# A two-stage Strassen MLP behind an attention and SSD block: sums and transposes laid into the output projection, the first and last two up pairs run product by product, low parts of W_down taken from PSUM, left sides of the down projection in half tiles

## The chip, the cores and the metric

The kernel runs on one core of a Trainium2 chip. The metric is the device time of one execution in microseconds (us), the median of several runs.

## The reference

One decoder block on x of 1024 rows and 1024 columns, all in float32. Only the end of it matters here:

```python
h1 = x + mix @ w_out                        # output projection, K = 2048
h  = rmsnorm(h1, norm_mlp_w)
u  = jnp.square(jax.nn.relu(h @ w_up))      # 1024 -> 4096
h2 = h1 + u @ w_down                        # 4096 -> 1024
y  = rmsnorm(h2, norm_final_w)
```

`mix` is the concatenation of the outputs of 16 state-space heads and 16 attention heads.

## The kernel before

All large products run as three passes of a rounded format: an operand is split into a high part (a cast on ScalarE) and a low part (the operand less its high part, a subtraction on VectorE or GpSimd), and high by high, high by low and low by high are added up in PSUM. `parts` (line 1179) is this split: `ac.copy` writes the high part, `low_by.tensor_tensor(... ALU.subtract)` the low part.

Both MLP products use one level of Strassen's method in Winograd's form: seven products in place of eight, with sums of quarters ahead and behind. Tokens are halved into rows 0 to 3 and 4 to 7 (tiles of 128 rows), K and columns are halved too.

- **Output projection** (`oproj_jobs`, line 827). Four groups `eg` of four K tiles; for each token tile and each half of the columns 12 matmuls into a bank `po`, then VectorE adds the bank to `h1`. The matmuls are yielded one by one by the generator `body`, and `fill` (line 321) draws them; `after(n, fn)` puts a function behind n further draws.
- **Norm and right sides of up** (lines 1152 to 1190 and 1312 to 1345). `norm_rows` makes `hn` for four rows, `turn` transposes it on TensorE into a bank `nt_m`, `quarter` splits a quarter, and from the two token halves come `b11`, `b21`, `b22` and the sums `t1` to `t4` (tiles `g_...`, for which `ta`, `tb` and `cc` are steps). All of it stands behind the last `po`; pair 0's first two products stand between the halves.
- **Up** (lines 1199 to 1360). 16 pairs `p`; each loads two blocks of W_up, makes its seven left sides (`up_split`: sums `us_...` on GpSimd, splits `uo_...` on ScalarE and VectorE) and runs seven products of 12 matmuls of 128x512 each. Banks `pu_a`, `pu_b`, `pu_c` collect them; `relu` and square give the four quarters of u, GpSimd makes the three sums and one difference that the next stage needs as left sides, and all seven go to DRAM (`uc_d`), tile `uc` by tile.
- **Down** (lines 1363 to 1510). 8 chunks of 2 pairs by 4 row positions i are 32 slots. A slot (`down_mm`) runs seven products of 6 matmuls. Two slots ahead, `down_in` loads the left sides of both pairs (`ul`, 896 columns, 448 KB by the SyncE queue), casts them on ScalarE (`uh`) and subtracts in place; GpSimd does that for i = 0 to 2 and VectorE for i = 3. `down_split` makes the seven right sides of a pair of W_down: sums `ds_t` on GpSimd, then `parts` on ScalarE and VectorE (`do_t` for sums, `do_b` for raw quarters of `wsd`). There are 22 buffers for them, 14 of which a chunk uses, so that most of a chunk's splits wait until the last slot of the chunk ahead frees their buffers. Each product is read from its bank (`pn_a` to `pn_d`) by VectorE, which adds it to `h1b` or `acc`; `pn_a`, `pn_b` and `pn_c` are used twice in a slot, and the second product into a bank waits for the read of the first.
- Behind the last chunk `final` squares, scales and writes the rows.

Each engine works through its own queue in order. The order in a queue comes from a scheduler that takes the program's order and the engines' occupation into account; only stretches between `kept.add("t")` and `kept.discard("t")` hold TensorE to the program's order. Buffers and banks belong to tags with fixed counts (`BUFS` and `PBUFS`, lines 103 and 105: eight banks as d 2, s 3, t 2, v 1).

Of the kernel before, what the change touches and what calls it, by code (L numbers as in the profile page):

```python
# [45 lines left out]
def tile_hymba_block(  # L46
# [780 lines left out]
    def oproj_jobs(eg):  # L827
# [337 lines left out]
    def turn(nts, k, th):
        pt = ps(("s", "t")[k % 2], f"nt_m_{th}_{k}")
        for ti in range(4):
            te.transpose(pt[:, ti * P:(ti + 1) * P], nts[ti][:, k * P:(k + 1) * P], ident)
        return pt
# [13 lines left out]
    cc = []
    nts = norm_rows(0)
    for k in range(HK):
        cc.append(sb("q", [P, 2, 512], F32, f"cc{k}"))
# [55 lines left out]
    banks = {}  # L1242
    t1s = {}

    def up_first(p):

        a = banks[p, "a"] = ps("d", f"pu_a{p}")
        up_prod(a, p, "a11", "b11", True)
        t1s[p] = sb(("y", "y", "vt")[p % 3], [P, 512], F32, f"ut1_{p}")
        ac.copy(t1s[p], a)  # L1250

    def up_second(p):
        up_prod(banks[p, "a"], p, "a12", "b21", False)

    def up_rest(p, between):
        a = banks[p, "a"]
        t1 = t1s[p]
        st = [sb(("p", "p", "ws")[(4 * p + j) % 3], [P, 4, 2, P], F32, f"uc{p}_{j}") for j in range(4)]

        def view(m):  # L1260
            j = UM.index(m)
            return st[j // 2][:, :, j % 2, :]

        def v3(ap):
            return ap.rearrange("p (i t) -> p i t", t=P)

        def tmp(nm):
            return sb("t", [P, 512], F32, f"u{nm}_{p}")

        def act(dst, src):  # L1270
            ac.activation(dst, src, AF.Relu)
            ac.activation(dst, dst, AF.Square)

        b = ps("s", f"pu_b{p}")
        up_prod(b, p, "s2", "t2", True)
        u2 = tmp("u2")
        ve.tensor_tensor(out=u2, in0=b, in1=t1, op=ALU.add)
        if between is not None:
            between()
        ac.activation(view("a11"), v3(a), AF.Relu)  # L1280
        ac.activation(view("a11"), view("a11"), AF.Square)
        up_prod(b, p, "s3", "t3", False)
        u3 = tmp("u3")
        ve.tensor_tensor(out=u3, in0=b, in1=t1, op=ALU.add)
        c = ps("t", f"pu_c{p}")
        up_prod(c, p, "s1", "t1", True)
        ve.tensor_tensor(out=u3, in0=c, in1=u3, op=ALU.add)
        up_prod(b, p, "a22", "t4", False)
        ac.activation(u3, u3, AF.Relu)
        ac.activation(view("a22"), v3(u3), AF.Square)  # L1290
        c21 = tmp("c21")
        ve.tensor_tensor(out=c21, in0=b, in1=t1, op=ALU.add)
        ac.activation(c21, c21, AF.Relu)
        ac.activation(view("a12"), v3(c21), AF.Square)
        up_prod(c, p, "s4", "b22", False)
        ve.tensor_tensor(out=u2, in0=c, in1=u2, op=ALU.add)
        act(u2, u2)
        a21 = v3(u2)
        gp.tensor_tensor(out=view("s3"), in0=view("a11"), in1=a21, op=ALU.subtract)
        gp.tensor_tensor(out=view("s1"), in0=a21, in1=view("a22"), op=ALU.add)  # L1300
        gp.tensor_tensor(out=view("s2"), in0=view("s1"), in1=view("a11"), op=ALU.subtract)
        gp.tensor_tensor(out=view("s4"), in0=view("a12"), in1=view("s2"), op=ALU.subtract)
        for j in range(4):
            n = min(2, 7 - 2 * j)
            sy.dma_start(out=uc_d[p][:, :, 2 * j:2 * j + n, :], in_=st[j][:, :, 0:n, :])
# [232 lines left out]
```

## Time and profile before

| | us |
|---|---|
| median of 3 runs | 1770.62 (1768.61 to 1771.44) |
| profiled execution, its own time | 1766.85 |
| its span | 1765.0 |
| TensorE busy in the span | 1632.2 (92%) |
| VectorE busy | 1211.0 (69%) |
| ScalarE busy | 763.7 (43%) |
| GpSimd busy | 779.0 (44%) |

In the profile the engines are PE (TensorE matmul), PEld (TensorE weight load), DVE (VectorE), ACT (ScalarE), POOL (GpSimd) and SP (SyncE, which issues the DMAs). All instructions are issued through one wrapper, so every row names line 85 and groups are told apart by their tiles. In a timeline the bracket behind a row is the idle time ahead of it and what ended that. The output projection ends at 1027.1, up at 1366.5, down at 1753.8.

### The profile page before, as it was taken

What the parts mean: (1) busy time and instruction counts of PE and PEld (TensorE: products, weight loads), DVE (VectorE), ACT (ScalarE), POOL (GpSimd) and SP (SyncE); (2) the same over time, 40 slices, a digit from 0 to 9 for tenths busy, and PEclk for the clock granted to TensorE, in tenths of its full rate; (3) what the DMA queues carried; (4) which work ended last, traced back from release to release, by engine and by line L of the source; (5) the groups of instructions that cost most, each with busy time, mean ns of one, the idle gap of its engine ahead of it and who ended that gap; (6) DMA issues with size and microseconds to landing.
All of it is one profiled execution on the core that took longest, in us unless ns stands there. A gap on an engine that the chain in (4) does not pass through costs nothing.

```text
span 1765.0 us, 22987 instructions
## 1 busy us (share of the span) xinstructions
PE 1632.2 (92%) x7994; PEld 1349.6 (76%) x7994; DVE 1211.0 (69%) x2082; ACT 763.7 (43%) x1610; POOL 779.0 (44%) x788
## 2 busy tenths in 40 slices
PE   7999898899999999999999968999999599888896
PEld 7887687778888888887888857888887477666775
DVE  5666867567777776777855466655655888888864
ACT  4223444335555555556411255455455333333333
POOL 4233553354333443443201145544544855556547
PEclk9999999999999999999999989999999799999998
DMA  5122334431112111103432322554555633333223
GB/s 172 42 58 63 93 84 100 83 82 32 35 34 46 35 35 32 44 27 125 148 105 86 107 84 74 165 155 138 160 162 195 228 122 132 131 116 123 102 96 121
DMA packets 171068, 175.38 MB, mean 99 GB/s; under 512 B 43364, under 2 KB 143928, under 8 KB 170952
## 3 DMA queue, kind: packets, MB, share of 16 engines
q1 hardware_dynamic: 169784, 173.12, 32.6%
q8 instruction: 63, 1.03, 0.3%
q0 software_dynamic: 1024, 0.53, 0.1%
q14 instruction: 53, 0.43, 0.1%
q10 hardware_dynamic: 144, 0.26, 0.0%
HBM read 127.15 MB, written 46.73 MB: 99 GB/s over the span
## 4 chain that ended last, share of the span: by engine, by line
PE 63%; DVE 11%; DMA 8%; issue 5%; ACT 5%; POOL 4%; SPq 0%; POOLq 0%; DVEq 0%; ACTq 0%
PE po L85 9%; PE pj_qk L85 8%; PE pu_b L85 7%; PE pj_v L85 5%; DMA eb<-cum_d 5%; PE pu_c L85 5%; PE pu_a L85 4%; PE s L85 4%; PE o L85 3%; PE tp L85 3%; PE pj_x L85 3%; PE pn_a L85 3%; PE pn_b L85 2%; DVE do_t L85 2%; PE pn_c L85 2%
## 5 line engine op out<-in xcount | busy, mean ns | idle before, releaser
L85 POOL TENSOR_SCALAR p<-p,rs 128x512 f32<-128x512 f32 (+2 forms) x144 | 102.9, 720 | 247.1 <-DVE rs L85 135.9
L85 PE MATMUL po<-wh_o,yy 128*128 128x512 f32 x512 | 161.8, 393 | 0.4 <-DVE k L85 0.4
L85 ACT ACTIVATE p<-s,mx 128x512 f32<-128x512 f32 (+1 forms) x192 | 110.4, 579 | 89.6 <-DVE mx L85 69.3
L85 ACT CAST uh<-ul 128x896 fp32r<-128x896 f32 x64 | 60.2, 942 | 179.0 <-DMA ul<-uc_d 166.2
L85 POOL TENSOR_TENSOR ul<-ul,uh 128x896 fp32r<-128x896 f32 x48 | 112.9, 2361 | 54.0 <-ACT uh L85 53.7
L85 DVE TENSOR_TENSOR pl<-tp,ph 128x512 fp32r<-128x512 f32 x192 | 105.9, 553 | 38.1 <-ACT ph L85 34.9
L85 ACT CAST ph<-tp 128x512 fp32r<-128x512 f32 x192 | 91.7, 478 | 70.0 <-PE tp L85 69.7
L85 PEld LDWEIGHTS po<-wh_o,yy 128*128 128x128 f32 x512 | 95.4, 188 | 19.4 <-DVE k L85 0.7
L85 PE MATMUL pj_qk<-hh,wl_qk 128*128 128x512 f32 x256 | 106.2, 415 | 0.0
L85 PE MATMUL pj_qk<-hl,wh_qk 128*128 128x512 f32 x256 | 105.9, 414 | 0.0
L85 PE MATMUL pj_qk<-hh,wh_qk 128*128 128x512 f32 x256 | 103.4, 404 | 0.0
L85 PE MATMUL s<-k,q 68*128 68x512 f32 (+7 forms) x384 | 101.9, 347 | 1.1 <-ACT p L85 0.9
L85 PE MATMUL po<-wl_o,yy 128*128 128x512 f32 x256 | 100.6, 393 | 0.0
L85 PE MATMUL pu_b<-g_t,uo_s 128*128 128x512 f32 x384 | 93.9, 394 | 4.0 <-DVE uu L85 4.0
L85 PE MATMUL tp<-ident,p 128*128 128x128 f32 x576 | 95.2, 273 | 1.2 <-POOL p L85 1.2
L85 PE MATMUL pu_a<-g_b,uo_a 128*128 128x512 f32 x384 | 94.5, 396 | 1.4 <-ACT ut L85 1.4
L85 DVE TENSOR_TENSOR do_t<-ds_t,do_t 128x512 fp32r<-128x512 f32 x64 | 91.6, 1433 | 5.6 <-ACT do_t L85 5.5
L85 PE MATMUL pz<-wh_z,hh 128*128 128x256 f32 (+1 forms) x256 | 76.9, 300 | 14.0 <-DVE z L85 11.4
L85 DVE TENSOR_TENSOR uo_s<-us_s,uo_s 128x512 fp32r<-128x512 f32 x64 | 61.9, 968 | 38.9 <-ACT uo_s L85 38.7
L85 PEld LDWEIGHTS pu_b<-g_t,uo_s 128*128 128x128 f32 x384 | 73.0, 191 | 20.0 <-DVE uu L85 3.5
L85 PEld LDWEIGHTS tp<-ident,p 128*128 128x128 f32 x576 | 72.6, 140 | 20.0 <-POOL p L85 2.6
L85 PEld LDWEIGHTS pu_a<-g_b,uo_a 128*128 128x128 f32 x384 | 73.1, 191 | 17.5 <-ACT ut L85 2.3
(293 smaller groups left out, 4721.4 us busy)
## 6 DMA issues: line engine op xcount, KB each, us to landing
ul<-uc_d SPq DMA_DIRECT2D x64, 448.0 KB, 4.0
uc_d<-uc SPq DMA_DIRECT2D x48, 512.0 KB, 3.2
ws_up<-in_w_up_dram SPq DMA_DIRECT2D x32, 512.0 KB, 3.8
wsd<-in_w_down_dram SPq DMA_DIRECT2D x32, 512.0 KB, 3.4
eb<-cum_d SPq DMA_DIRECT2D x16, 512.0 KB, 8.6
ws_qk<-in_w_in_dram SPq DMA_DIRECT2D x32, 256.0 KB, 3.6
wso<-in_w_out_dram SPq DMA_DIRECT2D x16, 512.0 KB, 3.4
yr<-yT_d SPq DMA_DIRECT2D x32, 256.0 KB, 2.7
```

Of the source, the lines that this page charges most:

```text
L85: i = call(*args, **kw)
```

## The change

- The last group of the output projection is drawn with other work between its matmuls. `norm_row` makes a row's norm as soon as its second half has been added; from row 3 on, the transposes and splits of the first token half (`left`, eight pieces), six splits of W_up for pairs 0 and 1, and the first half of the right sides' transposes and sums (`right_turn`, `right_sums`) are put behind counted draws. TensorE is held to program order from the middle of this group to the end of pair 1, and `po` has two banks there instead of five.
- Pairs 0 and 1 run product by product together, in the order p1, p2, p6, p7, p5, p4, p3; the sums t1 to t4 are made between them, t1's and t3's low parts on DVE. The last two pairs run together too, with p5 ahead of p7.
- A pair's result a22 is no longer copied into a `uc` tile but written to DRAM from the tile it is made in (`uu3`).
- From the second chunk on, a right side of W_down is cast twice on ACT: once into SBUF (the high part) and once into a PSUM bank `hb` (tag s); the low part is SBUF operand less PSUM bank, on DVE. `pn_b` moves to the two banks t and `pn_c` to d.
- The left sides come as half tiles `ui` (products 0 to 3 and 4 to 6 of a slot; high and low part in one tile), in a ring of 10 tiles over the tags q, p and ws, and all their low parts are made on POOL.

Its core:

```diff
@@ up
-    drain()
...
+    oproj_jobs(EG - 1, row)
+    fill(2 * (EG - 2) * NT * 3 * EG + NT * 3 * EG)
+    kept.add("t")
+    drain()
+    for p in range(2):
+        ups[p] = Up(p, "dts")
+    ups[0].p1()
+    ups[1].p1()
+    for k in range(HK):
+        right_turn(k, 1)
+    for k in range(HK):
+        right_sums(k, 1)
+        parts(gtile("t2", k), ta[k][:, 1, :], ve)
+    ups[0].p2()
+    ups[1].p2()
+    ups[0].p6()
+    ups[1].p6()
...
+        parts(gtile("t3", k), tb[k], ve)
...
+        parts(gtile("t1", k), ta[k][:, 0, :], ve)
...
+    ups[0].p7()
+    ups[1].p7()
...
+    for p in range(2, NPAIR - 2):
         up_load(p)
...
+    tails = [Up(p) for p in (NPAIR - 2, NPAIR - 1)]
...
+    for m in ("p1", "p2", "p6", "p5", "p7", "p4", "p3"):
+        for u in tails:
+            up_split(u.p, OP[m], True)
+        for u in tails:
+            getattr(u, m)()
@@ down_split
-            parts(o, src[m], ve)
+            if p < CP:
+                parts(o, src[m], ve)
+            else:
+
+                hb = ps("s", f"hb_{m}_{p}")
+                ac.copy(hb.bitcast(F32R), src[m])
+                ac.copy(o[:, 0], src[m])
+                ve.tensor_tensor(out=o[:, 1], in0=src[m], in1=hb, op=ALU.subtract)
@@ down_in
-            sy.dma_start(out=r32(lo), in_=uc_d[p][:, i])
-            ac.copy(hi, r32(lo))
-            (gp if i % 4 < 3 else ve).tensor_tensor(out=lo, in0=r32(lo), in1=r32(hi), op=ALU.subtract)
-            us_in[p, i] = hi, lo
+        for a, b in ((0, 4), (4, 7)):
+            for p in range(c * CP, (c + 1) * CP):
+                o = sb(uring[nu[0] % len(uring)], [P, 2, b - a, P], F32R, f"ui{p}_{i}_{a}")
+                nu[0] += 1
+                sy.dma_start(out=r32(o[:, 1]), in_=uc_d[p][:, i, a:b])
+                ac.copy(o[:, 0], r32(o[:, 1]))
+                gp.tensor_tensor(out=o[:, 1], in0=r32(o[:, 1]), in1=r32(o[:, 0]), op=ALU.subtract)
+                us_in[p, i, a // 4] = o
@@ down_mm
-        bb = ps("s", f"pn_b{nm}")
+        bb = ps("t", f"pn_b{nm}")
...
-        bc = ps("t", f"pn_c{nm}")
+        bc = ps("d", f"pn_c{nm}")
```

**Where instructions move.** At the start of up, on DVE, `g_t1` and `g_t3` are the low parts of the sums t1 and t3, `tb` the sum t3 itself, `uu2` the read of a p6 product. Before, k by k, each t3 follows its t2:

```order
L85 SCALAR_TENSOR_TENSOR ta1_10577<-nt_m_1_1_10570,prm_92,cc1_10390 128x512
L85 SCALAR_TENSOR_TENSOR ta1_10577<-nt_m_1_5_10579,prm_92,ta1_10577 128x512
L85 SCALAR_TENSOR_TENSOR tb1_0_10588<-nt_m_1_5_10579,prm_92,c12_1_10575 128x512
L85 TENSOR_TENSOR g_t2_1_10585<-ta1_10577,g_t2_1_10585 128x512
L85 TENSOR_TENSOR g_t3_1_10591<-tb1_0_10588,g_t3_1_10591 128x512
```

After the change, between the reads of pair 0's and pair 1's p6 and the product p7 (which needs t3):

```order
L85 TENSOR_TENSOR uu2_0_10682<-pu_b0_10669,ut1_0_10580 128x512
L85 TENSOR_TENSOR g_t1_2_10739<-ta2_10526,g_t1_2_10739 128x512
L85 TENSOR_TENSOR g_t1_3_10744<-ta3_10545,g_t1_3_10744 128x512
L85 TENSOR_TENSOR uo_s1_1_10796<-us_s1_1_10794,uo_s1_1_10796 128x512
L85 TENSOR_TENSOR uu2_1_10697<-pu_b1_10684,ut1_1_10595 128x512
L85 SCALAR_TENSOR_TENSOR tb0_3_10699<-nt_r4_10476,prm_92,cc0_10309 128x512
L85 SCALAR_TENSOR_TENSOR tb1_3_10709<-nt_r5_10500,prm_92,cc1_10348 128x512
L85 SCALAR_TENSOR_TENSOR tb2_3_10719<-nt_r6_10521,prm_92,cc2_10385 128x512
L85 TENSOR_TENSOR g_t3_0_10701<-tb0_3_10699,g_t3_0_10701 128x512
```

The parts of t1, which p5 uses, now stand ahead of those of t3, which TensorE's queue uses first, in p7.

On SP, where up gives over to down: `uc_d15` is the write of pair 15's left sides, `ui1_1_0` the load of pair 1's first half for the second slot. Before (`ul1_1` is the load for that slot):

```order
L85 DMA ul0_0_13101<-uc_d0_10447 128x896
L85 DMA uc_d15_10462<-uc15_0_12929 512x1x256
L85 DMA uc_d15_10462<-uc15_1_12930 512x1x256
L85 DMA uc_d15_10462<-uc15_2_12931 512x1x256
L85 DMA ul1_0_13106<-uc_d1_10448 128x896
L85 DMA ul1_1_13120<-uc_d1_10448 128x896
```

After:

```order
L85 DMA uc_d14_9461<-uc14_2_12933 512x1x256
L85 DMA uc_d15_9462<-uc15_0_12790 512x1x256
L85 DMA uc_d15_9462<-uc15_1_13000 512x1x256
L85 DMA uc_d15_9462<-uc15_2_12949 512x1x256
L85 DMA ui0_1_0_13095<-uc_d0_9447 128x512
L85 DMA ui1_1_0_13099<-uc_d1_9448 128x512
L85 DMA ui0_1_4_13103<-uc_d0_9447 128x384
L85 DMA ui1_1_4_13107<-uc_d1_9448 128x384
```

Slot 0's loads have moved ahead of the last writes (further up in the queue), slot 1's all stand behind them.

On DVE, in the last slot of chunk 3 and the first of chunk 4, before:

```order
L85 TENSOR_TENSOR do_t1_9_14387<-ds_t1_9_14385,do_t1_9_14387 128x512
L85 TENSOR_TENSOR h1b_3_13129<-h1b_3_13129,pn_a3_3_14319 128x512
L85 TENSOR_TENSOR do_t2_9_14397<-ds_t2_9_14395,do_t2_9_14397 128x512
L85 TENSOR_TENSOR h1b_7_13131<-h1b_7_13131,pn_b3_3_14327 128x512
L85 TENSOR_TENSOR do_t3_9_14392<-ds_t3_9_14390,do_t3_9_14392 128x512
```

After:

```order
L85 TENSOR_TENSOR do_t1_9_14571<-ds_t1_9_14569,hb_t1_9_14572 128x512
L85 TENSOR_TENSOR h1b_3_13119<-h1b_3_13119,pn_a3_3_14495 128x512
L85 TENSOR_TENSOR do_t3_9_14578<-ds_t3_9_14576,hb_t3_9_14579 128x512
L85 TENSOR_TENSOR do_t2_9_14585<-ds_t2_9_14583,hb_t2_9_14586 128x512
L85 TENSOR_TENSOR h1b_7_13121<-h1b_7_13121,pn_b3_3_14503 128x512
```

The subtractions and the reads take turns as before; the second operand of a subtraction is the bank `hb`.

## Rows read from the trace of the kernel before

**Rows 1.** Busy time by stage: stretch in us, its length, then busy us (and records) of PE, PEld, DVE, ACT and POOL, the granted clock, the share of the DMA engines and GB/s.

```profile
1027.10:1100.00 72.90, 54.15 (x234) 42.95 (x233) 50.50 (x62) 44.31 (x78) 37.90 (x31) 0.88 0.20 65
1100.00:1340.00 240.00, 240.00 (x1060) 198.75 (x1059) 142.68 (x165) 121.74 (x202) 121.59 (x88) 1.00 0.50 154
...
1366.50:1394.00 27.50, 8.58 (x19) 5.52 (x20) 25.01 (x18) 12.43 (x21) 25.76 (x16) 0.57 0.72 268
1394.00:1704.00 310.00, 276.68 (x1159) 220.46 (x1159) 257.48 (x295) 103.64 (x153) 171.47 (x93) 0.97 0.36 122
1704.00:1754.00 50.00, 44.34 (x169) 34.04 (x167) 26.66 (x40) 19.03 (x39) 36.31 (x39) 0.90 0.35 119
```

**Rows 2.** Timeline of PE at the start of up: start, length, instructions, and the idle time ahead with what ended it.

```profile
1027.12 2.35 PE L85 MATMUL nt_m<-ident,hn 128*128 128x128 f32 x20
...
1057.60 1.09 PE L85 MATMUL nt_m<-ident,hn 128*128 128x128 f32 x4 [4.07 <-DVE g_b L85]
...
1072.59 4.46 PE L85 MATMUL pu_b<-g_t,uo_s 128*128 128x512 f32 x12 [3.11 <-DVE uu L85]
```

**Rows 3.** Timeline of PE where up gives over to down.

```profile
1365.66 0.84 PE L85 MATMUL pu_c<-g_b,uo_s 128*128 128x512 f32 x3
1375.96 1.22 PE L85 MATMUL pn_a<-do_b,uh 128*128 128x512 f32 x2 [9.46 <-ACT uh L85]
1382.48 0.80 PE L85 MATMUL pn_a<-do_b,ul 128*128 128x512 f32 x1 [5.31 <-POOL ul L85]
1386.39 1.22 PE L85 MATMUL pn_a<-do_b,uh 128*128 128x512 f32 x2 [3.11 <-ACT uh L85]
...
1393.83 0.62 PE L85 MATMUL pn_a<-do_t,uh 128*128 128x512 f32 x2
```

**Rows 4.** Timeline of PE in down: the matmul with the idle time at the end of a chunk's first product, for the second and the seventh chunk, and the last row of all.

```profile
1432.67 0.50 PE L85 MATMUL pn_a<-do_b,ul 128*128 128x512 f32 x1 [2.28 <-POOL ul L85]
...
1661.02 0.50 PE L85 MATMUL pn_a<-do_b,ul 128*128 128x512 f32 x1 [1.64 <-POOL ul L85]
...
1753.39 0.39 PE L85 MATMUL pn_c<-do_t,ul 128*128 128x512 f32 x1
```

**Rows 5.** Groups of instructions from 1394 to 1704: engine, operation, tiles, count, busy us and mean ns of one, idle time ahead.

```profile
L85 POOL TENSOR_TENSOR ul<-ul,uh 128x896 fp32r<-128x896 f32 x40 | 94.8, 2377 | 46.4 <-ACT uh L85 46.2
L85 DVE TENSOR_TENSOR do_t<-ds_t,do_t 128x512 fp32r<-128x512 f32 x54 | 77.6, 1437 | 5.0 <-ACT do_t L85 4.9
...
L85 DVE TENSOR_TENSOR do_b<-wsd,do_b 128x512 fp32r<-128x512 f32 x40 | 55.0, 1377 | 0.0
L85 ACT CAST uh<-ul 128x896 fp32r<-128x896 f32 x54 | 51.0, 944 | 158.3 <-DMA ul<-uc_d 147.0 <-DVE h1b L85 7.6 <-PE pn_a L85 3.6
...
L85 DVE TENSOR_TENSOR h1b<-h1b,pn_b 128x512 f32<-128x512 f32 x54 | 36.7, 680 | 13.7 <-PE pn_b L85 13.7
...
L85 POOL TENSOR_TENSOR ds_t<-wsd 128x512 f32<-128x512 f32 x13 | 21.7, 1670 | 1.3 <-DVE do_t L85 1.3
...
L85 DVE TENSOR_TENSOR ul<-ul,uh 128x896 fp32r<-128x896 f32 x14 | 15.2, 1088 | 0.7 <-ACT uh L85 0.6
```

**Rows 6.** Timeline of DVE in down: around the turn from chunk 0 to chunk 1, and in a middle slot of chunk 1 (last row).

```profile
1424.36 2.03 DVE L85 TENSOR_TENSOR do_t<-ds_t,do_t 128x512 fp32r<-128x512 f32 x1
1426.30 0.68 DVE L85 TENSOR_TENSOR h1b<-h1b,pn_c 128x512 f32<-128x512 f32 x1
...
1446.26 0.68 DVE L85 TENSOR_TENSOR do_b<-wsd,do_b 128x512 fp32r<-128x512 f32 x1
1446.86 0.68 DVE L85 TENSOR_TENSOR h1b<-h1b,pn_d 128x512 f32<-128x512 f32 x1
...
1455.04 0.69 DVE L85 TENSOR_TENSOR h1b<-h1b,pn_b 128x512 f32<-128x512 f32 x1 [0.67 <-PE pn_b L85]
```

**Rows 7.** Timeline of ACT around the turn from chunk 0 to 1.

```profile
1423.24 1.66 ACT L85 CAST do_t<-ds_t 128x512 fp32r<-128x512 f32 x3
...
1425.33 0.57 ACT L85 COPY acc<-pn_a 128x512 f32<-128x512 f32 x1
```

**Rows 8.** The page's DMA issues: count, KB each, median us from issue to landing.

```profile
ul<-uc_d SPq DMA_DIRECT2D x64, 448.0 KB, 4.0
uc_d<-uc SPq DMA_DIRECT2D x48, 512.0 KB, 3.2
```

**Rows 9.** Timeline of POOL where up gives over to down.

```profile
1365.26 1.30 POOL L85 TENSOR_TENSOR ds_t<-wsd 128x512 f32<-128x512 f32 x1 [0.71 <-DVE do_t L85]
...
1371.56 1.71 POOL L85 TENSOR_TENSOR uc<-uc,uu 128x512 f32<-128x512 f32 x1
```

**Rows 10.** Groups of instructions from 1027.1 to 1100, as in rows 5.

```profile
L85 DVE TENSOR_TENSOR g_t<-tb,g_t 128x512 fp32r<-128x512 f32 x4 | 6.9, 1730 | 0.1
...
L85 ACT ACTIVATE cc<-nt_m,prm 128x512 f32<-128x512 f32 x8 | 5.8, 735 | 0.0
...
L85 DVE SCALAR_TENSOR_TENSOR tb<-nt_m,prm,c 128x512 f32<-128x512 f32 x4 | 3.0, 743 | 0.0
```

**Rows 11.** Timeline of PE in the last chunk, the three longest idle times.

```profile
1719.90 0.73 PE L85 MATMUL pn_a<-do_t,uh 128*128 128x512 f32 x2 [2.01 <-DVE h1b L85]
1729.62 0.73 PE L85 MATMUL pn_a<-do_b,uh 128*128 128x512 f32 x2 [1.70 <-ACT uh L85]
1731.79 0.79 PE L85 MATMUL pn_a<-do_b,ul 128*128 128x512 f32 x1 [1.43 <-POOL ul L85]
```

More of the change, by code (lines that the diff above doesn't have):

```diff
@@ L825, in tile_hymba_block, with oproj_jobs @@
     h1 = {}
-    def oproj_jobs(eg):
+    def oproj_jobs(eg, row=None):
         w = []
@@ L1241, in tile_hymba_block @@
     UM = ("a11", "s1", "s3", "s2", "a12", "s4", "a22")
[L1242 to L1305, printed above, removed]
@@ new lines, in tile_hymba_block, with row @@
+    OP = {"p1": "a11", "p2": "a12", "p6": "s2", "p7": "s3", "p5": "s1", "p4": "a22", "p3": "s4"}
+    ups = {}
+    def row(tt, dh):
+        norm_row(tt, dh)
+        if dh == 1 and tt == 3:
+            for p in range(2):
+                up_load(p)
+            for j in range(2 * HK):
+                after(24 + 5 * j, lambda j=j: left(j))
+            for n, (p, m) in enumerate(((0, "a11"), (1, "a11"), (0, "a12"), (1, "a12"), (0, "s2"), (1, "s2"))):
+                after(34 + 9 * n, lambda p=p, m=m: up_split(p, m, True))
+            for k in range(HK):
+                after(72 + 5 * k, lambda k=k: (right_turn(k, 0), right_sums(k, 0)))
@@ new lines, in tile_hymba_block @@
+    for k in range(HK):
+        parts(gtile("t1", k), ta[k][:, 0, :], ve)
+        tb[k] = sb("t", [P, 512], F32, f"tb{k}_4")
+        gp.tensor_tensor(out=tb[k], in0=cc[k][:, 1, :], in1=ta[k][:, 1, :], op=ALU.subtract)
+    ups[0].p7()
+    ups[1].p7()
+    for k in range(HK):
+        quarter("b22", k, p22[k], mlpw(k + HK))
+    for p in range(2):
+        up_split(p, "s1", True)
+    ups[0].p5()
+    ups[1].p5()
+    for k in range(HK):
+        parts(gtile("t4", k), tb[k], gp)
+    for m, pr in (("a22", "p4"), ("s4", "p3")):
+        for p in range(2):
+            up_split(p, m, True)
+        for p in range(2):
+            getattr(ups[p], pr)()
@@ L1424, in prod @@
                     te.matmul(
-                        bank, us_in[p, i][x][:, j, :], w[:, y, :], start=first and n == 1,
+                        bank, u[:, x, j % 4, :], w[:, y, :], start=first and n == 1,
                         stop=n == total, skip_group_check=True,
@@ L1488, in tile_hymba_block @@
     for i in range(4):
+        if i < 2:
+            down_in(0, i)
         for tt in (i, i + 4):
@@ L1499, in tile_hymba_block @@
             down_load((c + 1) * CP + i // 2)
+        if wfb is None and c == NCH - 1:
+            wfb = sb("v", [P, D], F32, "wfb")
+            sy.dma_start(out=wfb, in_=norm_final_w.partition_broadcast(P))
         down_mm(c, i)
```

282 lines of the change are left out of this document (173 added, 109 removed).

## The prediction

> **What bounds the kernel now.** I first read the busy time by stage, because the share of the whole span hides three different limits. In the middle of up PE is never idle: 1060 matmuls in 240.00 us at a granted clock of 1.00 [rows 1], which is 0.2264 us per matmul and the floor for all that follows. Up and down have 1344 matmuls each, 304.3 us; a product is 12 (2.72 us) in up and 6 (1.36 us) in down; a chunk of down is 168, 38.0 us. Against that floor I count what each stretch loses.
>
> - Start of up. From the first transposes at 1027.12 [rows 2] to the end of up at 1365.66 + 0.84 = 1366.50 [rows 3] are 339.4 us. Less 304.3, and less 64 transposes at 2.35/20 (7.5 us), **27.6 us** are lost. All of it lies before 1100, where PE is busy 54.15 of 72.90 us at a mean clock of 0.88 [rows 1]; what ends its waits is DVE, which makes the sums [rows 2].
> - Up to down. From 1366.50 to 1393.83 run 18 matmuls (4.1 us), with waits of 9.46, 5.31 and 3.11 us for the left sides [rows 3]: **23.2 us** lost, part of it at the lower clock (mean 0.57 [rows 1]; 1.2 of 2.4 GHz would be 0.50).
> - Chunks 0 to 6. The same wait comes at 1432.67 and, five chunks later, at 1661.02 [rows 4]: 45.67 us per chunk in place of 38.0. From 1393.83 to the last matmul's end at 1753.78 are 360.0 us for 1326 matmuls (300.2): 59.8 us lost. The last chunk begins near 1661.02 + 45.67 = 1706.7 and takes 47.1 us for 166 matmuls (37.6), 9.5 lost, so the others lose **50.3 us**.
> - Behind 1753.78, 11.2 us of norm and writing, untouched by the change.
>
> Why do chunks lose 7.6 us? DVE is busy 257.48 of 310 us [rows 1]. Its groups show two prices for 128x512: 680 ns where one operand is a bank (h1b from pn_b), but 1437 and 1377 ns for the low parts do_t and do_b, whose operands both lie in SBUF [rows 5]. The timeline shows that these have two speeds: 2.03 us at 1424.36 and 0.68 us at 1446.26, while the read right behind either takes 0.68 [rows 6]. GpSimd's subtractions are the obvious partner. In the middle slots DVE waits for each product, at a step of 1.36 us (idle 0.67 ahead of the read [rows 6]): there PE is the bound. In the last slot of a chunk and the first of the next (19.0 us of PE), where buffers come free, 14 low parts at 1.4 us stand among 14 reads: 14 x 1.41 + 14 x 0.60 (the step from 1446.26 to 1446.86 [rows 6]) + 2 `ul` at 1.09 [rows 5] = 30.3 us. DVE is the bound there; of the 11.3 us over PE's 19.0, 7.6 show, since some of it reaches into the neighbouring slots.
>
> **Part by part.** *Low parts from PSUM.* The new subtraction has the operands of a read, one tile and one bank: 0.68 us, step 0.60. The two slots then need 28 x 0.60 = 16.8 of 19.0 us, and the `ul` of DVE are gone. The price is 14 more ACT casts per chunk. The trace has no SBUF to PSUM cast; the nearest rows are SBUF to SBUF, 1.66 us for three (0.55 each), and PSUM to SBUF, 0.57 for one [rows 7]. ACT's work in the two slots is 28 x 0.55 = 15.4, plus the casts of four loads at 0.94 [rows 5], with some 0.1 for cutting each in two, 4.2: 19.6 of 19.0 us. So ACT is level with PE where DVE was far above it, and DVE's reads stand in its queue behind subtractions that wait for ACT. A bank used twice allows for this: between the end of a slot's first product and the start of its fourth lie two products, 2.7 us, and a lag of 0.6 us fits.
>
> The page "ScalarE: Activation LUTs" of the Trainium skill, section "Step-by-step: what each stage is for", says that ScalarE writes to PSUM faster than to SBUF; no row here shows it. By it the added casts lie below 0.55, ACT stays under 19.0, and of the 12 us below some 3 would be left: 1704, within the span of the forecast.
>
> *Half tiles.* Before, a slot's loads wait for the slot two ahead of it to end, one slot (9.5 us) of lead for 4.0 us of landing [rows 8], 0.94 of cast and 2.38 of subtraction [rows 5] for each of two pairs. With ten half tiles the first halves reuse tiles freed at the end of the slot three ahead, the second halves those freed after the fourth product of the slot two ahead, each some 19 us before use. The waits at the chunk's first product [rows 4] should go. POOL now makes all of them: 8 x 2.38 = 19.0 and 8 sums at 1.30 [rows 9] to 1.67 [rows 5], 29 to 32 of 38.0 us per chunk: room enough.
>
> "GPSIMD Engine Reference", section 4.1 Engine selection, of the Trainium skill speaks against this: elementwise work with two inputs belongs on VectorE, since GpSimd takes about twice as long. The rows agree, 2377 against 1088 ns for the same tile [rows 5]. By the rule the two moved subtractions take 2.6 us more on POOL than they took on DVE; left on DVE, the last chunk could lose that much less, and the sum would be 1710.
>
> I take 1.7 us of loss per chunk for what is left (a late ACT cast ahead of a read): **12 us** for seven chunks; bounds 3 (0.4 per chunk, reads always in time) and 30 (4.3, ACT as the bound, below). Gain 38.
>
> *Start of up.* The sums of the first half and 48 of 64 transposes move between the matmuls of the last `po` group. After the last `po` (call it 0) p1 of two pairs gives 5.4 us, in which row 7 is normed; 16 transposes end at 7.3, p2 at 12.8, p6 at 18.2. DVE then has for p6: eight half sums and four `g_t2`, and up to 15.5 that fits. But before t3 it makes the four `g_t1` and `uo_s1`, then reads p6, then four `tb` at 0.74 and four `g_t3` [rows 10]. From 15.5: five low parts at 1.0 (between 0.68 and 1.73 [rows 6, 10]), two reads at 0.69, four `tb` (3.0), two `uo_a22` (2.0), four `g_t3` (4.0) end at 31. p7 wants the first of these at 18.2 and the last 2.0 later: a stall of about 10 us. With a slow clock behind it I take **13.5 us** (bounds 8: the low parts at 0.68; 20: at 1.73). Gain 14.
>
> *Last `po` group.* There PE is full now, and 48 transposes stand in its fixed order, waiting for banks which ACT must empty: 16 casts at 0.71 to 0.74 (cc [rows 10]) with splits and norms, about 20 us of ACT work beside 27 us of PE. I take **2.5 us** of stall (bounds 0 and 8, PE waiting 0.7 for each of the last pieces).
>
> *Up to down.* Slot 0's left sides and the splits of chunk 0 now lie under the last products: the 9.46 us are gone. But all loads of slot 1 stand in SP's queue behind the writes of pair 15, which wait for POOL: after the last product (T), ten instructions at 1.30 to 1.71 [rows 9], 13 to 17 us. Then the load, 4.0 [rows 8], a cast and two half subtractions (2.7): slot 1 can begin at T + 22, and slot 0 ends at T + 9.5. 12.5 us of stall, 1.5 for the second halves, and some 3 at the lower clock: **17 us** (bounds 10, POOL ahead by two instructions and the clock kept; 25, the writes' 3.2 us [rows 8] and POOL at 1.71 throughout). Gain 6.
>
> *Last chunk.* Waits of 2.01, 1.70 and 1.43 us [rows 11] come from full queues, and POOL's grows: **10 us** as before (bounds 8 and 14). Middle pairs of up stay at PE's floor, since DVE, ACT and POOL have 40% and more to spare there [rows 1].
>
> Sum: 27.6 + 23.2 + 50.3 + 9.5 = 110.6 us lost now; 13.5 + 17 + 12 + 10 + 2.5 = 55.0 after. Gain 55.6, from the profiled execution's own time 1766.85: 1711.2. That execution lies 3.8 us under the median; the runs of the new kernel may lie between, and I say **1713**.
>
> **Rivals.**
> - *A, all covers hold* (every term near its lower end, 29 lost): 1685 to 1697. For it: DVE's low parts have been seen at 0.68. Against: the two queue orders, on DVE and SP, which are fixed.
> - *B, ACT takes DVE's place.* If a cast into PSUM doesn't overlap with the next and costs 0.62 or more, ACT needs 22 us for 19 and a chunk 41.5: steady loss 25, time 1726. For it: 19.6 of 19.0. Against: ACT idles 158 us for loads in this stretch [rows 5], so its other work can move.
> - *C, the change doesn't do what it says:* a subtraction with a bank still takes 1.4 us. Then the two slots need 28.1, 2.2 less than now, a chunk about 43.5, steady loss 38: 1739. Against: 54 reads at 680 ns beside a busy POOL [rows 5].
> - *D, slower.* In the two slots every subtraction waits for two casts, and the next read behind it; if each of 14 right sides holds PE by 1.0 us more, a chunk costs 14 more, 98 in all: 1811. It decides from 0.57 us each (55.6/98), beyond the 2.7 us that the banks allow. Before, the same order with slower subtractions cost 7.6 per chunk, which speaks against it.
> - *E, the joint of up and down at its upper end* (SP's queue): 1721 to 1733.
>
> **How the numbers follow.** The forecast, 1697 to 1721, has 0.45; A 0.15; B 0.20; E 0.10; C 0.04; D 0.04; no change 0.02. A measurement tells 0.2%, 3.5 us, from no change. All but D and no change are faster: 0.94, 0.02, 0.04. The range 1690 to 1740 leaves out half of A, C's end, D and no change.
>
> **What would show it.** Right: `do` low parts at 0.68 to 0.70 whatever POOL does; PE steps of about 39.7 us per chunk; a wait of about 10 us at the first p7, ended by DVE's `g_t3`; one of about 12 at slot 1, ended by `ui1_1` and SP's writes. Wrong: subtractions at 1.4 us; a chunk above 42; PE waits inside the last `po` group of more than 8 us; a slot 0 that waits as now.

## The result, and the profile after

The changed kernel takes 1703.68 us (median of 4 runs, 1701.5 to 1707.26) where the kernel before takes 1769.61 beside it (1765.88 to 1771.44): a ratio of 0.9632, interval 0.9607 to 0.9657. The prediction of 1713 had the sign, the mechanism and the range; it was 9 us too high, and terms that were too small and too large cancel in it (below). The profiled execution took 1701.5 us, its span 1699.7, at the same 11 us of tail as before.

First the windows of the kernel after, against [rows 1] (columns as there: window, length, busy time of PE, PEld, DVE, ACT, POOL, granted clock, DMA share, GB/s). They are the last `po` group, the start of up, the turn from up to down, the chunks behind it (from the middle of the first on), and the last chunk:

```profile
1010.00:1040.00 30.00, 25.14 (x126) 19.94 (x125) 20.36 (x32) 18.09 (x33) 12.86 (x14) 0.94 0.24 89
1040.00:1100.00 60.00, 54.99 (x232) 43.87 (x231) 44.07 (x60) 35.67 (x64) 32.58 (x26) 0.94 0.28 88
1358.00:1394.00 36.00, 20.54 (x78) 15.59 (x79) 15.76 (x23) 17.82 (x35) 25.83 (x22) 0.81 0.70 244
1394.00:1650.00 256.00, 255.74 (x1129) 211.42 (x1128) 178.23 (x277) 153.73 (x292) 192.53 (x165) 1.00 0.48 151
1650.00:1689.00 39.00, 32.98 (x135) 24.31 (x133) 18.91 (x27) 16.16 (x40) 32.05 (x40) 1.00 0.30 105
```

In the chunks PE is busy 255.74 of 256 us at a granted clock of 1.00: TensorE's floor. What is left to lose lies in the four short stretches around. Their waits, from the timeline of PE of the kernel after (start, duration, row, and in the bracket the idle time ahead and what ended it):

```profile
1021.84 1.11 PE L85 MATMUL nt_l<-ident,hn 128*128 128x128 f32 x4 [3.90 <-ACT cc L85]
...
1061.08 0.50 PE L85 MATMUL pu_b<-g_t,uo_s 128*128 128x512 f32 x1 [2.09 <-ACT g_t L85]
...
1068.60 5.08 PE L85 MATMUL pu_b<-g_t,uo_s 128*128 128x512 f32 x14 [2.16 <-DVE g_t L85]
...
1360.57 1.66 PE L85 MATMUL pn_b<-do_t,ui 128*128 128x512 f32 x6 [2.64 <-DVE uu L85]
...
1382.08 3.44 PE L85 MATMUL pn_a<-do_b,ui 128*128 128x512 f32 x6 [11.34 <-ACT ui L85]
...
1671.08 1.65 PE L85 MATMUL pn_a<-do_t,ui 128*128 128x512 f32 x6 [2.00 <-DVE h1b L85]
```

With the landmarks of this timeline (first `pu_a` at 1040.48, first `pn_a` at 1356.41, a slot each time `pn_a` takes `do_b` anew, end at 1688.5) and the floor of 0.2264 us per matmul, the account by stage is:

| lost against the floor, us | before | predicted (bounds) | after |
|---|---|---|---|
| last `po` group, with 48 transposes in it | 0 | 2.5 (0 to 8) | 6.9 |
| start of up | 27.6 | 13.5 (8 to 20) | 9.7 |
| up to down | 23.2 | 17 (10 to 25) | 19.3 |
| chunks | 50.3 | 12 (3 to 30) | 0.3 |
| last chunk | 9.5 | 10 (8 to 14) | 8.2 |
| sum | 110.6 | 55.0 | 44.4 |

For the kernel after, the third row holds the turn and all of chunk 0 (57.4 us, floor 38.04), the fourth chunks 1 to 6; the kernel before cut in that way has 24.6, 46.7 and 11.7 in rows three to five. The predicted 12 were for seven chunks; 10.2 of them fall to these six. The sum falls by 66.2; the part ahead of the last `po` group was 0.8 longer, and 65.3 us is the difference of the spans.

The terms of the chunks in the kernel after, 1394 to 1650, grouped by form (count, busy, mean ns, idle ahead; against [rows 5]):

```profile
L85 DVE TENSOR_TENSOR do_t<-ds_t,hb_t 128x512 fp32r<-128x512 f32 x52 | 35.0, 683 | 6.7 <-ACT hb_t L85 5.5 <-PE pn_a L85 0.6
L85 DVE TENSOR_TENSOR do_b<-wsd,hb_b 128x512 fp32r<-128x512 f32 x39 | 26.5, 682 | 3.5 <-ACT hb_b L85 3.5
L85 ACT CAST do_t<-ds_t 128x512 fp32r<-128x512 f32 x52 | 32.1, 620 | 10.0 <-PE pn_a L85 9.7
L85 ACT CAST hb_t<-ds_t 128x512 fp32r<-128x512 f32 x52 | 29.8, 581 | 4.6 <-POOL ds_t L85 4.5
L85 POOL TENSOR_TENSOR ds_t<-wsd,ds_t 128x512 f32<-128x512 f32 x26 | 33.8, 1298 | 6.3 <-DVE do_t L85 5.7
```

The low parts fell from 1437 and 1377 ns to 683 and 682. ACT is as full as it was feared in the first and the last slot of a chunk; the windows of the four slots of chunk 2 show it (ACT's busy time is 9.52, 3.66, 2.28 and 8.47 us):

```profile
1451.86:1461.38 9.52, 9.52 (x43) 7.88 (x42) 8.67 (x15) 9.52 (x20) 8.74 (x8) 1.00 0.69 236
1461.38:1470.90 9.52, 9.52 (x43) 7.88 (x42) 4.82 (x7) 3.66 (x7) 6.92 (x8) 1.00 0.50 158
1470.90:1480.40 9.50, 9.50 (x43) 7.88 (x42) 4.82 (x7) 2.28 (x4) 4.70 (x6) 1.00 0.31 97
1480.40:1489.92 9.52, 9.52 (x43) 7.88 (x42) 8.65 (x14) 8.47 (x17) 8.56 (x8) 1.00 0.49 151
```

### The profile page after: what moved, and what is told of

Its sections match the earlier page's. It is cut to its first block, busy times and chain, and to the rows that moved or that the text cites. A ratio compares the mean times of both kernels' runs of the same rounds, so it can differ in the third digit from the quotient of the medians.

```text
span 1699.7 us, 23561 instructions
## 1 busy us (share of the span) xinstructions
PE 1614.2 (95%) x7994; PEld 1341.5 (79%) x7994; DVE 1113.4 (66%) x2074; ACT 821.6 (48%) x1778; POOL 803.6 (47%) x873
## 4 chain that ended last, share of the span: by engine, by line
PE 69%; DVE 7%; DMA 7%; POOL 6%; ACT 4%; issue 4%; SPq 0%; POOLq 0%; DVEq 0%; ACTq 0%
PE po L85 9%; PE pj_qk L85 9%; PE pu_b L85 6%; PE pj_v L85 5%; DMA eb<-cum_d 5%; PE pn_a L85 4%; PE pu_c L85 4%; PE pn_b L85 4%; PE pn_c L85 4%; PE pu_a L85 4%; PE s L85 4%; PE o L85 4%; PE tp L85 3%; PE pj_x L85 3%; PE pn_d L85 2%
## 5 line engine op out<-in xcount | busy, mean ns | idle before, releaser
L85 POOL TENSOR_TENSOR ui<-ui 128x384 fp32r<-128x384 f32 (+1 forms) x128 | 145.9, 1161 | 64.9 <-ACT ui L85 51.2
L85 ACT CAST ui<-ui 128x384 fp32r<-128x384 f32 (+1 forms) x128 | 71.5, 566 | 104.2 <-DMA ui<-uc_d 102.6
L85 PE MATMUL pn_c<-do_t,ui 128*128 128x512 f32 x384 | 97.8, 390 | 0.8 <-DVE h1b L85 0.8
L85 PEld LDWEIGHTS s<-k,q 128*128 128x128 f32 (+1 forms) x384 | 70.8, 188 | 20.2 <-ACT p L85 4.8
L85 PEld LDWEIGHTS pn_c<-do_t,ui 128*128 128x128 f32 x384 | 71.9, 188 | 16.6 <-DVE h1b L85 1.6
```

The source lines that it names most:

```text
L85: i = call(*args, **kw)
```

## The experiments

Each ratio is to the kernel before on the same chip, with its 95% interval. The kernel before took 1773.92 beside experiments 1, 2, 3 and 5, 1768.41 beside 4, 6, 7 and 8, and 1769.27 beside 9 to 12.

**1. The bank taken back.** All right sides are split from SBUF again, the rest of the change stays:

```diff
-            if p < CP:
+            if True:
```

> The changed kernel with one part undone: every right side of W_down is split from SBUF alone again (one cast on ACT, the subtraction with two SBUF operands on DVE); banks, half tiles and all else stay. Theory P (the subtraction with a bank as an operand doesn't meet POOL, and this carries the steady gain): the low parts take 1.3 to 1.5 us on average again, a chunk of down takes 43 to 45 us in place of 38.1, and the time is 1704 + 6 to 7 chunks x 5 to 7 = 1737 to 1752. Rival H (the half tiles' lead carries the gain, DVE's longer low parts hide under PE): the low parts are as long, but a chunk stays under 39.5 and the time under 1714.

1732.27 us, 0.9756 (0.9728 to 0.9784). It lies between the two: less was lost than theory P said, far more than rival H. Chunk 1 takes 44.8 us, chunks 2 to 6 take 41.5 to 42.4, not 38.08 and not 45.67. The groups of this kernel, 1425 to 1675:

```profile
L85 DVE TENSOR_TENSOR do_t<-ds_t,do_t 128x512 fp32r<-128x512 f32 x48 | 56.3, 1175 | 3.9 <-ACT do_t L85 3.9
...
L85 POOL TENSOR_TENSOR ds_t<-wsd,ds_t 128x512 f32<-128x512 f32 x24 | 38.5, 1606 | 9.4 <-DVE do_t L85 5.3 <-DMA ui<-uc_d 3.6
```

The subtraction is slow again, and the sums on POOL beside it are slower too (1606 against 1298 ns). With POOL making all left low parts DVE has 2 `ul` fewer per chunk, and a low part costs 1175 ns where it cost 1437, so its two slots hold less. POOL is busier here than in the kernel before (201.24 of 250 us against 171.47 of 310 [rows 1]), so the share of its busy time alone doesn't set the price; see experiment 4.

**2. Whole tiles again.** Left sides of 896 columns in a ring of two tags, POOL still makes them all, the bank stays:

```diff
-        for a, b in ((0, 4), (4, 7)):
-            for p in range(c * CP, (c + 1) * CP):
...
+        for p in range(c * CP, (c + 1) * CP):
+            tag = "qp"[nu[0] % 8 // 4]
```

> The changed kernel with one part undone: the left sides of down come as whole tiles of 896 columns in the old ring of eight (high and low tile of both pairs, two slots), all low parts on POOL; low parts of W_down still from the bank. Theory P: the lead is one slot, 9.5 us, against 4.0 of landing, 0.94 of cast and 2 x 2.1 of subtraction for two pairs, about 9.9 with the second cast, so each slot waits up to 1 us, or 1.6 to 2.3 once per chunk as before the change: 1711 to 1730. Rival N: with DVE out of POOL's way the loads are in time on one slot of lead: within 3 us of 1704.

1715.05 us, 0.9668 (0.9641 to 0.9695). The time is the one that theory P gave, but not for its reason, a wait in every slot or chunk: chunks 1 to 6 take 38.08 all the same, but for one of 38.5. What it loses lies in chunk 0 (65.4 us against 57.4) and in the last chunk (50.6 against 46.3; PE waits of 3.02, 1.43 and 3.12 us). So the half tiles are not what makes the chunks fast.

**3. The bank alone, in the kernel before.** The new branch of `down_split` and the moved tags of `pn_b` and `pn_c`, nothing else:

```diff
-            parts(o, src[m], ve)
+            if p < CP:
+                parts(o, src[m], ve)
+            else:
+                hb = ps("s", f"hb_{m}_{p}")
...
-        bb = ps("s", f"pn_b{nm}")
+        bb = ps("t", f"pn_b{nm}")
```

> The kernel before with one part of the change alone: low parts of W_down from the bank (with the moves of pn_b to tag t and pn_c to tag d that it needs); left sides in whole tiles, VectorE's share of their low parts and all of up as before. Theory P: DVE's low parts at 0.68, a chunk from 45.7 to 38.5 to 40.5 (the wait at the chunk's first product stays at about 1.7), 1770 - 36 to 48 = 1722 to 1734. Rival H: less than 15 us gained. Rival B (ACT takes DVE's place): a chunk at 41 to 43, 1740 to 1750.

1723.8 us, 0.9713 (0.9693 to 0.9732), 50.1 less than before. Chunk 1 takes 39.5 us, chunks 2 to 6 take 38.08 to 38.10. Its groups, 1434 to 1663:

```profile
L85 POOL TENSOR_TENSOR ul<-ul,uh 128x896 fp32r<-128x896 f32 x37 | 78.6, 2131 | 37.2 <-ACT uh L85 37.2
...
L85 DVE TENSOR_TENSOR do_t<-ds_t,hb_t 128x512 fp32r<-128x512 f32 x48 | 32.2, 681 | 0.0
```

POOL gains as well: its 896-column subtraction takes 2131 where it took 2377 ns [rows 5].

**4. Is it POOL that slows the subtraction?** As in 1, and POOL's subtraction of the left sides is left out, so that down's result is another one:

```diff
-                gp.tensor_tensor(out=o[:, 1], in0=r32(o[:, 1]), in1=r32(o[:, 0]), op=ALU.subtract)
```

> As bank_undone (low parts of W_down from two SBUF operands), and POOL's subtraction for the left sides of down is left out: the loaded value stands in the place of its low part, so the result of down is another. Theory P (POOL is what slows the subtractions with two SBUF operands): low parts of W_down at 0.68 to 0.95 on average in chunks 1 to 6 (only the sums of W_down are left on POOL), a chunk at 38.1 to 39.0. Rival T (two SBUF operands are slow in themselves, or ACT sets the pace): 1.3 us or more, a chunk at 41 or more.

1707.84 us (2 runs), 0.9662 (0.9637 to 0.9687). POOL's busy time from 1416 to 1652 falls to 63.38 of 236 us, and the groups of that stretch read

```profile
L85 DVE TENSOR_TENSOR do_t<-ds_t,do_t 128x512 fp32r<-128x512 f32 x49 | 46.0, 941 | 4.2 <-ACT do_t L85 4.2
L85 DVE TENSOR_TENSOR do_b<-wsd,do_b 128x512 fp32r<-128x512 f32 x36 | 34.9, 969 | 0.0
```

The same instruction on the same operands: 1437 ns in the kernel before, 1175 in experiment 1, 941 with most of POOL's work gone, 683 with one operand in a bank. Chunk 1 takes 40.3 us, chunks 2 to 6 take 39.0 to 39.4. POOL's traffic is the cause.

Single instructions of the kernel before say the same without a second run. The 2.03 us at 1424.36 [rows 6] lie beside POOL's 896 columns, the 0.68 at 1446.26 in a gap of POOL:

```profile
1423.42 2.41 POOL L85 TENSOR_TENSOR ul<-ul,uh 128x896 fp32r<-128x896 f32 x1
...
1440.11 5.08 POOL L85 TENSOR_TENSOR ul<-ul,uh 128x896 fp32r<-128x896 f32 x2
1446.77 1.32 POOL L85 TENSOR_TENSOR ds_t<-wsd,wsd 128x512 f32<-128x512 f32 x1 [1.58 <-DMA wsd<-in_w_down_dram]
```

Of the 93 low parts on record in the window of [rows 5], the 18 that POOL overlaps for less than half of their length take 677 to 693 ns. The other 75 take 1591 on average: 2021 where most of the overlap is with 896 columns, 1362 where it is with the sums of 512. In the kernel after, the 78 that POOL overlaps for half or more take 678 to 689. So the price goes by which instruction of POOL runs beside. That accounts for a part of experiment 1, where POOL has no 896 columns; that the low parts beside its sums take 1205 there and not 1362 stays open.

**5. Slot 1 loaded early.** Its loads go to buffers that are free before pair 15's writes are issued:

```diff
-    uring = ["q"] * 4 + ["p"] * 4 + ["ws"] * 2
+    uring = ["q"] * 8 + ["ws"] * 2
...
-            h1[tt] = sb("q", [P, D], F32, f"h1b_{tt}")
+            h1[tt] = sb("q" if i < 2 else "p", [P, D], F32, f"h1b_{tt}")
```

> The changed kernel with other buffers at the turn from up to down: the ring of half tiles is eight q and two ws, and four of the h1b tiles that are needed last take the p buffers of the last pairs in their place, so that slot 1's loads need no buffer that pair 15's writes must free. Theory S (SP's queue behind POOL's last sums holds slot 1): slot 1 starts within 2 us of slot 0's end, 11 to 16 us less, 1688 to 1693. Rival Q (POOL's own queue, or the loads' transfer beside the writes, holds slot 1 as long): slot 1 still waits 7 us or more, 1697 to 1704.

1705.11 us, 0.9616 (0.9589 to 0.9644). Neither theory came true: the 11.34 us wait is gone, but chunk 0 takes 58.3 us in place of 57.4: slot 0 now takes 14.2 and slot 1 21.9. The wait has gone to DVE, whose queue holds splits of chunk 1 ahead of the reads that free PE's banks; a later read waits 3.98 us for a load of `h1b` behind the writes. From its timeline, DVE, then PE:

```profile
1374.82 0.69 DVE L85 TENSOR_TENSOR do_t<-ds_t,hb_t 128x512 fp32r<-128x512 f32 x1 [5.15 <-ACT hb_t L85]
```

```profile
1378.39 2.93 PE L85 MATMUL pn_c<-do_t,ui 128*128 128x512 f32 x6 [4.14 <-DVE h1b L85]
```

**6. t3 ahead of the reads of p6.** Two sums and low parts of t3 are put in front of pair 0's p6, two in front of pair 1's:

```diff
+    for p in range(2):
+        up_split(p, "s3", True)
+    kept.add("v")
...
-            up_split(k, "s3", True)
+        if k == 1:
+            ups[0].p6()
+    ups[1].p6()
```

> The changed kernel with another order on DVE at the start of up: the low parts of t3 for k = 0 and 1 stand ahead of the read of pair 0's p6, those for k = 2 and 3 ahead of the read of pair 1's, and the splits for s3 ahead of all (held to program order from the right sums to the second p6). Theory O (the order, t1 ahead of t3, causes the waits of 2.09, 0.76 and 2.16 us at p7 and the slow clock behind them): these waits fall below 1 us in all, 4 to 7 us less, ratio to the kernel before 0.959 to 0.961 where the changed kernel has 0.963. Rival W (DVE has too much work there in any order): a wait of the same size at p5 or p4, or at p6, and less than 2 us gained.

1704.08 us, 0.9643 (0.9626 to 0.966). Nothing is gained, as rival W had it. The first `pu_a` to the first `pn_a` takes 317.05 us against 315.93, which isn't told from no change: kernels of this study that leave up's start alone have 315.9 to 317.2. At p7 the waits for `g_t` shrink to 0.83 and less, but 2.88 us appear for pair 1, ended by DVE's read of p6. The DVE work ahead of p7 is the same in either order.

**7. POOL held to program order in the last `po` group**, so that the steps of a row's norm don't stand behind sums `us_s`:

```diff
-    kept.add("t")
+    kept.update("tg")
...
+    kept.discard("g")
```

> The changed kernel with POOL held to program order in the last group of the output projection, so that the sums of the W_up splits stand behind the small steps of a row's norm and not between them. Theory V (DVE's norm of row 4 waits for POOL's two small steps, between which a sum of 1.3 us stands, and ScalarE and TensorE wait for the bank reads queued behind it on DVE): the wait of 3.90 us at 1021.84 falls below 1 us, and with it the stretch at the lower clock: 5 to 7 us less, ratio 0.959 to 0.961. Rival U (ACT itself is late, with splits and squares ahead of the reads): a wait of 2 us or more stays in this group, less than 2 us gained.

1703.84 us, 0.9638 (0.962 to 0.9656). The 3.90 us wait is gone, waits of 1.82 and 1.52 for the second half's transposes take some of its place; first transpose to first `pu_a` takes 26.28 us against 29.11. This is between theory V and rival U: 2.8 us gained in the stage, which the median doesn't show: the last matmul of attention alone comes at 888.4 to 896.5 us in the profiled executions of this study, a scatter larger than that.

**8. The turn in the order in which it is needed.** As in 5, and POOL works off pair 14's sums, slot 1's first halves, pair 15's sums, then the rest, with p3 cut into product and sums:

```diff
+    down_in(0, 0)
+    tail(("p4", "p3"))
+    h1_load(0)
+    h1_load(1)
+    kept.add("g")
+    tails[0].p3b()
+    down_in(0, 1, ((0, 4),))
+    tails[1].p3b()
+    down_in(0, 1, ((4, 7),))
```

> As slot1_early, and POOL held to program order at the turn: pair 14's last sums, first halves for slot 1, pair 15's, second halves for slot 1, the left sides of slots 2 and 3, and only then the sums for pairs 2 and 3 of W_down; both h1b tiles of slot 1 are loaded ahead of the writes. In slot1_early the reads of slot 0 stood on DVE behind subtractions for pair 2 that waited for POOL (5.15 us), and slot 1's second h1b tile behind the writes. Theory S2 (these two are what ate slot1_early's gain): slots 0 to 2 follow within 4 us of waits in all, chunk 0 loses 5 to 9 us in place of 19.3, ratio 0.955 to 0.958. Rival L (the work only moves): pairs 2 and 3 are late, chunk 1 starts with waits of 5 us or more, ratio 0.961 or above.

1703.28 us, 0.9641 (0.9619 to 0.9662). Slot 1 starts without a wait, slot 2 waits for its loads, which now stand behind the writes; chunk 0 takes 55.8 us, where theory S2 had 43 to 47, and chunk 1, at 38.08, isn't late, against rival L. PE, then SP's queue:

```profile
1389.17 1.22 PE L85 MATMUL pn_a<-do_b,ui 128*128 128x512 f32 x2 [6.29 <-ACT ui L85]
```

```profile
1367.20 10.98 SPq L85 DMA_DIRECT2D uc_d<-uc  x6
1381.17 6.97 SPq L85 DMA_DIRECT2D ui<-uc_d  x8
```

**9. Slot 2's first halves ahead of the writes too.** As in 8. Buffers for them come from tag p, `h1b` of rows 2 and 6 from p, of 3 and 7 from ws; the low parts of the later halves stand behind pair 15's sums, and `pu_c` of the last two pairs moves to tag s:

```diff
+    later_low = []
+    down_in(0, 1, ((0, 4),))
+    down_in(0, 1, ((4, 7),), later_low)
+    down_in(0, 2, ((0, 4),), later_low)
+    tails[1].p3b()
```

> As turn_in_order, with the loads for slot 2 freed from pair 15's writes: the ring is eight q and two p, the two p being pair 14's; the loads for slot 2's first halves stand in SP's queue ahead of pair 15's writes; the h1b tiles of slots 2 and 3 take what pair 15 leaves; and the last two pairs collect pu_c in the banks s, so that pn_b of slot 0 doesn't wait for its read. Theory S3 (slot 2's wait of 6.3 us in turn_in_order is again a buffer that pair 15's writes must free): slots 0 to 3 run with under 4 us of waits, chunk 0 takes 42 to 46 us in place of 57.4, ratio to the kernel before 0.956 to 0.958. Rival M (POOL's own work sets the end of chunk 0: eight sums for pairs 2 and 3 stand last): chunk 0 or 1 waits 5 us or more for right sides, together 84 us or more in place of 95.5, ratio 0.959 to 0.961.

1697.53 us, 0.96 (0.958 to 0.962). Chunk 0 takes 52.5 us, where theory S3 had 42 to 46. The loads no longer bind; waits of 2.90, 2.02 and 2.74 us for DVE's reads are what is late next, and the longest wait ahead of those reads on DVE is again for a cast of a right side of chunk 1:

```profile
1392.27 0.69 DVE L85 TENSOR_TENSOR do_t<-ds_t,hb_t 128x512 fp32r<-128x512 f32 x1 [5.41 <-ACT hb_t L85]
```

**10. The last chunk's additions of `acc` on DVE:**

```diff
-                gp.tensor_tensor(out=dst, in0=dst, in1=acc[i], op=ALU.add)
+                ve.tensor_tensor(out=dst, in0=dst, in1=acc[i], op=ALU.add)
```

> The changed kernel, with the three additions of acc to the h1b halves in each slot of the last chunk on DVE in place of POOL. Theory A (POOL's queue in the last chunk holds DVE's reads, and its three additions of 3.7 us stand between the last products and the end): the last chunk loses 3 to 6 us in place of 8.2 and the tail behind the last matmul takes 9 to 10 in place of 11.2: 4 to 7 us less, ratio 0.959 to 0.961. Rival D (DVE is held by its own queue, and two SBUF operands meet POOL): within 2 us, 0.962 to 0.964.

1701.64 us, 0.9622 (0.96 to 0.9645). The last chunk takes 42.21 us against 46.28; the tail stays at 11.06, where theory A had 9 to 10. The median falls by 1.7 us alone beside the changed kernel of experiment 12, as rival D had it; the 4.1 us are read from the length of the stage. So half of the last chunk's 8.2 us was POOL, which in the kernel after needs 3.79 us for three such additions.

**11. Experiments 7, 9 and 10 together:**

> turn_ring, last_adds_dve and pool_in_order in one kernel. If their gains add: 12 to 18 us less than the changed kernel, ratio 0.952 to 0.956, with the join of up and down at 5 to 9 us lost and the last chunk at 3 to 6. If one covers another (the end of the last chunk waits for the same POOL work): 0.957 to 0.960.

1693.5 us (5 runs, 1689.53 to 1695.41), 0.9576 (0.9554 to 0.9598): faster than both kernels. Chunk 0 takes 51.2 us, the last chunk 42.2, first transpose to first `pu_a` 26.5. By these lengths the gains add up in full (6.2 + 4.1 + 2.6 = 12.9 us); the median is 9.9 below that of experiment 12, in the range that was named for gains that cover one another. The stages show no such cover; what lies ahead of the first transpose, which none of the three touches, is 4.1 us longer in its profiled execution than in that of experiment 12.

**12. The changed kernel once more, beside it:**

> The changed kernel once more beside the three others, so that they are compared on one chip: ratio to the kernel before within the interval seen, 0.961 to 0.966, and the same stretches: 29.1 us from the first transposes to the first up product, 315.9 to 317.1 us of up, 57.4 for chunk 0, 38.08 for each of chunks 1 to 6, 46.3 for the last.

1703.36 us (1701.17 to 1706.48), 0.9635 (0.9613 to 0.9657). First transpose to first `pu_a` 29.0, up 316.6, chunk 0 57.40, chunks 1 to 6 38.08 each, the last 46.22: the lengths of the stages of this kernel repeat to some 0.7 us where its runs scatter by 5.

## Why the prediction was right, and where it was off

**Low parts from PSUM: right mechanism, the term far too large** (12 taken for seven chunks, 10.2 of it for chunks 1 to 6, which lose 0.3; the lower bound was 3). The price of the subtraction was right (0.68; 683 measured). So was ACT's load: 19.6 us were worked out for the two slots, 9.52 + 8.47 = 18.0 are seen, with more in the slot behind. The step that failed is the margin of 1.7 us per chunk for casts that come late: PE's floor holds although ACT is full in slot 0. DVE waits 5.5 us for `hb_t` and 3.5 for `hb_b` in 256 us, and none of that reaches PE, which idles 0.26 us in that time; the prediction had worked out that two products, 2.7 us, lie between a bank's uses. Rivals B, C and D fall with it: chunks of 41.5, subtractions of 1.4 us, or waits behind two casts weren't there. The Trainium skill ("ScalarE: Activation LUTs", "Step-by-step: what each stage is for") has casts into PSUM as the faster ones; 581 against 620 ns agrees. No run shows what casts of 620 ns into the bank would have cost.

**What makes it work is that POOL and DVE no longer meet.** "GpSimd's subtractions are the obvious partner" was an inference; experiments 1 and 4 show it, POOL's sums being a partner as well, and 3 shows that POOL gains from it too. The Trainium skill ("SBUF — State Buffer", "Who interferes with whom") says that a DVE instruction with two SBUF inputs contends with a GpSimd instruction that reads SBUF, and one with a single SBUF input doesn't; the prices in experiment 4 agree, 677 to 693 ns without POOL and 1591 with it from two SBUF operands, 678 to 689 with it from one.

**How much of the 65 us is the bank's.** Alone it gives 50.1 (experiment 3); taken away from the whole change it makes down 28.6 us longer (first `pn_a` to the last matmul's end takes 360.7 in place of 332.1 us), or some 22 by the two ratios. Both are right: half tiles, POOL's share and the moved tags of `pn_b` and `pn_c`, which no run tells apart, bring a chunk from 45.67 to about 42 without the bank and add nothing to 38.08 with it. The prediction's paragraph on half tiles credited them with the chunk's first waits; experiment 3 has whole tiles and loses these waits too, and experiment 2 leaves the half tiles 12 us, in chunk 0 and in the last chunk.

**Start of up: the wait was where it was put, half as long.** 13.5 taken, 9.7 measured; at the first p7, 2.09 + 0.76 + 2.16 = 5.0 us in place of 10, the last ended by DVE's `g_t` as said. DVE was done with the last part of t3 28.1 us after the first `pu_a`, not 31: low parts taken at 1.0 us took 0.64 to 0.99. Beside the waits, 9 matmuls of p7 took 4.10 us in place of 2.04, at a granted clock of 0.58. Experiment 6 points to DVE's amount of work, not only to the order: what is taken from one wait comes back at the next read.

**Last `po` group: 6.9 in place of 2.5**, near its bound of 8. The term counted ACT's casts; the wait came from POOL, which the text didn't weigh there. The chain, from the timelines of ACT, DVE and POOL in the kernel after:

```profile
1021.10 0.69 ACT L85 ACTIVATE cc<-nt_l,prm 128x512 f32<-128x512 f32 x1 [3.54 <-DVE g_b L85]
```

```profile
1018.66 1.74 DVE L85 TENSOR_SCALAR hn<-h,v_m 128x1024 f32<-128x1024 f32 x1 [3.68 <-POOL v_m L85]
```

```profile
1016.56 0.19 POOL L85 TENSOR_SCALAR v_m<-ss_m 128x1 f32<-128x1 f32 x1
1016.83 1.29 POOL L85 TENSOR_TENSOR us_s<-ws_up 128x512 f32<-128x512 f32 x1
1018.08 0.55 POOL L85 TENSOR_TENSOR v_m<-v_m,mhalf 128x1 f32<-128x1 f32 x1
```

A step of 0.55 us stands behind a sum of 1.29 in POOL's queue, `hn` on DVE waits for it, DVE's low parts `g_b` stand behind `hn`, and ACT's `cc` and the transposes wait for those. Experiment 7 removes this wait.

**Up to down: 19.3 in place of 17, and the queue was the right one.** 11.34 us at slot 1 (12.5 predicted), with SP's six writes ahead of the loads as in experiment 8. That these are so close is luck: slot 1 began 25.7 us after the last product of up, not 22, as fourteen and not ten instructions stood in POOL's queue up to pair 15's last sum, and slot 0 ended after 14.3, not 9.5. Not foreseen in slot 0: 2.64 us at the second product, whose bank waits for DVE's read of the last product of up, and 1.42 at the fourth. Experiments 5, 8 and 9 show a chain of queues here: freed from SP's writes, the stretch is held by DVE's reads, which stand behind subtractions that wait for ACT. What would bring chunk 0 from 51 to 38 stays open.

**Last chunk: 8.2 in place of 10.** It was put down to full queues, POOL's growing; experiment 10 gives 4.1 us of it to POOL's additions. The rest, waits of 0.47, 1.47 and 1.14 us behind DVE's reads, was not taken apart, and no run has the two left sides of each chunk back on DVE.

**The sum.** The last `po` group and the turn were taken 6.7 us too small, the chunks, the start of up and the last chunk 17.3 too large: 55.0 against 44.4. The time came out closer than the terms because these partly cancel.

## What to carry to other kernels

A subtraction of two SBUF operands on VectorE beside a busy GpSimd is priced with the company it keeps: look for two speeds of one shape in the timeline, and if ScalarE has room, let it put one operand into a PSUM bank. At the joint of two stages, follow every queue (the DMA issues, too) past the wait that is removed, since the instruction queued behind it is what is late next. Gains of a few us are read in the length of their stage, and only their sum in the median.

## What the hardware showed that was not expected

- A subtraction with one operand in a bank costs no more than the best of two SBUF operands: 682 to 683 ns against 0.68 us [rows 6].
- A cast from SBUF into a bank takes 581 ns, into SBUF 620 ns, for 128x512.
- Both sides pay when the two engines meet: POOL's sums take 1606 ns beside slow subtractions and 1298 beside fast ones, its 896 columns 2377 and 2131 ns.
